# A decoder layer's output projection in pairs of token blocks by Strassen's product, with the layer norm on three engines

## The chip, the core and the metric

The kernel runs on one core of a Trainium2 chip. A core has TensorE (PE, with PEld for its weight loads), VectorE (DVE), ScalarE (ACT), GpSimd (POOL) and SyncE (SP, which here only issues DMAs). The metric is the device time of one execution in microseconds; it is 440.44 us before the change, the median of three runs (439.75 to 440.67).

## What is computed

One decoder layer for 1024 tokens of width 1024, all in float32. Cut to what matters:

```python
h = x @ w_in                                  # 1024 x 2368: six parts
x_q, x_kv, k_rope_raw, gate_a, u_pool, gate_b = split(h)
y_a = latent_attention(x_q, x_kv, k_rope_raw, positions, ...) * silu(gate_a)   # 4 heads, causal by position
y_b = pooling_mixer(u_pool, pool_w, pool_scale) * silu(gate_b)                 # windows 2, 4, 8, 16
mix = concatenate([y_a, y_b], axis=-1) @ w_out                                 # 1024 x 1024
x = layer_norm(alpha * x + mix, ln_g, ln_b)
```

The causal mask is by `positions`; where they rise strictly, a block of queries needs only the blocks of keys up to its own.

## The kernel before

**Precision.** Every matrix product is made of three fp32r matmuls: an operand is split into a high part (cast to fp32r, on ACT: `split`, line 419) and a low part (the rest, on DVE or, with `pool=True`, on POOL: `low`, line 415), and high·high, high·low and low·high are summed in PSUM. A split of a tile is thus one ACT cast and one subtraction.

**Stages.** `start` (line 373) loads positions, weights and x and makes a flag that says whether positions rise; the program branches on it (line 1277). The fast branch runs `in_projection` (with `gate_a` first), `up_projections`, `attention` and `out_projection`. The input projection already goes by Strassen's product in Winograd's form: eight rounds, each of which makes two column tiles from seven products of 12 matmuls (`multiply`, line 535); sums of x's quarters are made once (`right_sums`), sums of w_in's tiles in each round (`prepare`), and round i asks for the weights of round i+2 and prepares those of round i+1. The mixer's results go to DRAM (`yb_d`), as does silu of the gates (`silu_d`).

**Order.** Nothing is issued where it is written. Each call notes an operation in a `Planner` (line 86), which, before the build, lays out all operations of the branch by a list schedule: each engine takes, of what is ready within 30 ns of the soonest, what is written first, by costs set in `cost` (line 141). That fixes each engine's order and which buffer each tile gets: 13 pages of 128 x 1024 float32 (`F`, named m), 41 of the same size for split operands and others (`T`, named b), and six places in PSUM (`PS_KINDS`, a set for each stage). Tiles of a kind are handed out in the order of first use; a later one can go ahead only if enough are spare for all before it. All instructions therefore carry one line in the profile, L316, and groups are told by tile names and shapes.

**Output projection.** `out_projection` (line 1222) takes eight blocks of 128 tokens. For blocks 0 to 3 it goes through the eight row tiles of w_out (`wo_split`: load, split) and adds to four accumulators; then blocks 4 to 7 come one after the other. Per block and row tile `out_mm` issues three terms by two halves of 512 columns. The last block's second half is cut into two of 256. When a block is summed, `norm` (line 1179) does on DVE: alpha·x + sum, statistics, aggregate, epsilon; the power -1/2 on POOL; a centring and a scaling pass of 1024 on DVE; the store. The last block does these two passes in four pieces, one of which is scaled by ACT and POOL. During attention, `SIDE_AT` names the steps at which y_b's four tiles and w_out's first three are split, with the low parts on POOL.

Of the kernel before, what the change touches and what calls it, by code (L numbers as in the profile page):

```python
# [33 lines left out]
SIDE_AT = (9, 12, 16, 28, 20, 22, 29)  # L34
# [9 lines left out]
}  # L44
# [297 lines left out]
class Layer:  # L342
    def __init__(self, ctx, tc, d, out, plans):
# [20 lines left out]
        self.trig_d = dram.tile([32, 2, S], F32, name="trig_d")  # L364
        self.yb_d = [dram.tile([P, S], F32, name=f"yb_d{i}") for i in range(4)]
# [77 lines left out]
    def bank(self):  # L443
        kind = ("a1", "x1", "p1")[self.stage]
        return self.E.tile(self.ps, kind, len(PS_KINDS[kind][1]), [P, 512], F32)
# [11 lines left out]
    def run(self, ctx, full):  # L457
# [10 lines left out]
        E.tracked = {t.tensor.name for t in self.silu_d + self.yb_d + [self.trig_d]}  # L468
# [381 lines left out]
    def in_projection(self):  # L850
# [8 lines left out]
        for i, (n, _) in enumerate(self.PAIRS):  # L859
# [119 lines left out]
    def attention(self):  # L979
# [3 lines left out]
        self.ya, self.yb, self.wo, self.wo_raw = [None] * NH, [None] * NH, [None] * 8, {}  # L983
# [100 lines left out]
        def pv(h, g):  # L1084
# [12 lines left out]
            if self.ya[h] is None:  # L1097
                self.ya[h] = (self.T(), self.T())
            c = slice(g * GQ * 128, g * GQ * 128 + GQ * 128)
            y = self.silu_a[h][:, c]  # L1100
            self.mul(y, ps, y)
            self.split(self.ya[h][0][:, c], self.ya[h][1][:, c], y, pool=True)

        side = {}
        if not full:
            side = {}
            for t, job in zip(SIDE_AT, [(self.yb_split, g) for g in range(4)] + [(self.wo_split, n) for n in range(3)]):
# [37 lines left out]
        if full:  # L1145
            for g in range(4):
                self.yb_split(g)

# [7 lines left out]
    WO_ORDER = (4, 5, 6, 7, 0, 1, 2, 3)  # L1156

    def yb_split(self, g, pool=False):
        y = self.load(self.yb_d[g])
        self.yb[g] = (self.T(), self.T())  # L1160
        self.split(*self.yb[g], y, pool)

    def wo_split(self, n, pool=False):
        k = self.WO_ORDER[n]
        raw = self.load(self.d["w_out"][k])
        self.wo[k] = (self.T(), self.T())
        self.split(*self.wo[k], raw, pool)

    def out_mm(self, parts, s, n):
        k = self.WO_ORDER[n]  # L1170
        a, w = self.ya[k] if k < 4 else self.yb[k - 4], self.wo[k]
        for q, (i, j) in enumerate(((0, 0), (0, 1), (1, 0))):
            for f, c in parts:
                self.E.tensor.matmul(
                    f, a[i][:, s * 128 : s * 128 + 128], w[j][:, c],
                    start=(n == 0 and q == 0), stop=(n == 7 and q == 2),
                )

    def norm(self, s, parts, tail=False):
        E, small, ln_g, ln_b = self.E, self.small, self.ln_g, self.ln_b  # L1180
        z, o = self.xs.pop(s), self.F()
        b0 = 48 + 16 * (s % 2)
        mv, rs = small[:, b0 : b0 + 2], small[:, b0 + 2 : b0 + 3]
        stats = self.stats[:, 18 * (s % 2) : 18 * (s % 2) + 18]
        i = 0
        for f, c in parts:
            E.vector.scalar_tensor_tensor(out=o[:, c], in0=z[:, c], scalar=ALPHA, in1=f, op0=ALU.mult, op1=ALU.add)
            for n in range(c.start, c.stop, 512):
                E.vector.bn_stats(out=stats[:, 6 * i : 6 * i + 6], in_=o[:, n : min(n + 512, c.stop)])
                i += 1  # L1190
        E.vector.bn_aggr(out=mv, in_=stats[:, : 6 * i])
        E.vector.tensor_scalar(out=rs, in0=mv[:, 1:2], scalar1=LN_EPS, scalar2=None, op0=ALU.add)
        E.gpsimd.tensor_tensor(out=rs, in0=rs, in1=self.half[:, 0:1], op=ALU.pow)
        def center(c):
            E.vector.scalar_tensor_tensor(
                out=z[:, c], in0=o[:, c], scalar=mv[:, 0:1], in1=ln_g[:, c], op0=ALU.subtract, op1=ALU.mult
            )

        def scale(c, pool=False):
            if pool:  # L1200
                E.scalar.activation(o[:, c], z[:, c], AF.Identity, scale=rs)
                E.gpsimd.tensor_tensor(out=o[:, c], in0=o[:, c], in1=ln_b[:, c], op=ALU.add)
            else:
                E.vector.scalar_tensor_tensor(
                    out=o[:, c], in0=z[:, c], scalar=rs, in1=ln_b[:, c], op0=ALU.mult, op1=ALU.add
                )
            E.sync.dma_start(self.out[s * 128 : s * 128 + 128, c], o[:, c])

        if not tail:
# [12 lines left out]
    def out_projection(self):  # L1222
        E = self.E
        self.ln_g, self.ln_b = self.F(), self.F()
        E.sync.dma_start(self.ln_g, self.d["ln"][0:1, :].partition_broadcast(128))
        E.sync.dma_start(self.ln_b, self.d["ln"][1:2, :].partition_broadcast(128))
        self.xs = {}

        def x_load(s):
            if s < NB:  # L1230
                self.xs[s] = self.load(self.d["x"][s * 128 : s * 128 + 128, :])

        for s in range(3):
            x_load(s)
        accs = [self.acc() for _ in range(4)]
        for n in range(8):
            if n >= (0 if self.full else 3):
                self.wo_split(n)
# [126 lines left out]
```

## Time and profile before

| | |
|---|---|
| median of three runs | 440.44 us |
| the profiled execution, its own time | 439.69 us |
| its span, first to last instruction | 437.9 us |
| mean granted TensorE clock | 0.988 |
| PE busy | 424.9 us, 97% of the span, 2031 matmuls |
| DVE busy | 325.9 us, 74% |
| ACT busy | 187.1 us, 43% |
| POOL busy | 74.9 us, 17% |
| HBM read, written | 31.81 MB, 8.65 MB |
| PE's share of the chain that ended last | 87% |

Busy time is the time in which an engine had an instruction in work. Idle time of an engine that is not on the chain that ended last costs nothing by itself. Matmuls are pipelined, so their single durations overlap; a pitch is read from a stretch, as time over count. The same holds for DVE's short passes: the start of one to the start of the next is their pitch.

### The profile page before, as it was taken

The numbers are of one execution on the slowest core, as the hardware profiler recorded it, in microseconds if no ns is written. First come the engines' busy times: TensorE is split into PE (matmuls) and PEld (weight loads), VectorE is DVE, ScalarE is ACT, GpSimd is POOL, SyncE is SP. The second block draws the span as 40 slices with busy tenths as digits, with TensorE's granted clock in tenths as the row PEclk, the third lists the DMA queues.
The fourth block names the chain that finished last, engine by engine and source line by source line (L and its number), as shares of the span: only waits on it lengthen the run. The fifth ranks groups of instructions, "written<-read, shape, count | busy, mean of one in ns | idle before, by whom it ended". The sixth has DMA issues, their size and how long they took to land.

```text
span 437.9 us, 5669 instructions
## 1 busy us (share of the span) xinstructions
PE 424.9 (97%) x2031; PEld 356.4 (81%) x2031; DVE 325.9 (74%) x601; ACT 187.1 (43%) x338; POOL 74.9 (17%) x88
## 2 busy tenths in 40 slices
PE   6999999999999999999999999999999999999991
PEld 4888888888888888888788898989898888888881
DVE  4996996668688999838998679696969600299564
ACT  5755764243332436543333658596869200000000
POOL 0000001000010000000101116668483200024111
PEclk8999999999999999999999999999999999999996
DMA  8823522304023002514339101131447300032211
GB/s 287 334 97 99 214 100 93 97 0 145 0 105 101 0 23 66 179 63 128 120 79 214 68 1 49 50 97 52 157 144 265 106 1 0 0 136 106 96 49 56
DMA packets 14457, 43.53 MB, mean 99 GB/s; under 512 B 2133, under 2 KB 4309, under 8 KB 14421
## 3 DMA queue, kind: packets, MB, share of 16 engines
q1 hardware_dynamic: 14133, 42.57, 29.4%
q10 hardware_dynamic: 288, 0.52, 0.4%
q8 instruction: 18, 0.29, 0.3%
q14 instruction: 18, 0.15, 0.1%
HBM read 31.81 MB, written 8.65 MB: 92 GB/s over the span
## 4 chain that ended last, share of the span: by engine, by line
PE 87%; DVE 6%; DMA 4%; ACT 1%; issue 1%; DVEq 0%
PE p L316 49%; PE x L316 31%; PE a L316 7%; DVE m L316 3%; DMA m<-w_uq 3%; DVE b L316 2%; DMA pp<-pos_pair 1%; DVE small L316 1%; ACT m L316 0%; ACT b L316 0%; DVEq L400 0%; DVE stats L316 0%; DVE p L316 0%; PE psflag L396 0%; DVE cmp L389 0%
## 5 line engine op out<-in xcount | busy, mean ns | idle before, releaser
L316 PE MATMUL p<-b,b 128*128 128x512 f32 (+4 forms) x1032 | 220.9, 370 | 0.1
L316 PEld LDWEIGHTS p<-b,b 128*128 128x128 f32 x1032 | 181.2, 188 | 30.2 <-DVE b L316 0.4
L316 PE MATMUL x<-b,b 128*128 128x512 f32 x696 | 158.2, 389 | 0.0
L316 PEld LDWEIGHTS x<-b,b 128*128 128x128 f32 x696 | 130.6, 188 | 27.4 <-ACT m L316 0.4
L316 ACT CAST b<-m 128x1024 fp32r<-128x1024 f32 (+2 forms) x96 | 83.4, 898 | 51.3 <-DVE m L316 32.7
L316 DVE TENSOR_TENSOR b<-m,b 128x1024 fp32r<-128x1024 f32 (+3 forms) x91 | 84.2, 963 | 17.9 <-ACT b L316 17.8
L316 ACT CAST b<-p 128x256 fp32r<-128x256 f32 (+3 forms) x118 | 37.3, 385 | 29.8 <-PE p L316 29.5
L316 DVE TENSOR_TENSOR b<-p,b 128x256 fp32r<-128x256 f32 (+3 forms) x118 | 44.0, 419 | 6.2 <-ACT b L316 6.0
L316 DVE SCALAR_TENSOR_TENSOR m<-m,p 128x512 f32<-128x512 f32 (+2 forms) x13 | 10.2, 799 | 43.4 <-PE p L316 43.4
L316 POOL TENSOR_TENSOR small<-small,cst 128x1 f32<-128x1 f32 (+1 forms) x10 | 14.8, 1479 | 148.4 <-DVE small L316 148.4
L316 DVE TENSOR_TENSOR m<-m,m 128x512 f32<-128x512 f32 (+4 forms) x51 | 39.1, 788 | 1.4 <-ACT m L316 1.2
L316 ACT COPY m<-x 128x512 f32<-128x512 f32 x33 | 19.1, 586 | 48.5 <-PE x L316 41.4
L316 ACT ACTIVATE m<-m,small 128x320 f32<-128x320 f32 x1 | 0.6, 562 | 84.1 <-POOL small L316 84.1
L316 DVE TENSOR_TENSOR m<-m 128x512 f32<-128x512 f32 (+5 forms) x39 | 29.3, 761 | 4.7 <-ACT m L316 4.7
L316 POOL TENSOR_SCALAR m<-m,small 128x384 f32<-128x384 f32 (+7 forms) x32 | 24.0, 752 | 45.2 <-DVE small L316 36.8
L316 PE MATMUL a<-b,b 128*128 128x512 f32 x128 | 31.2, 406 | 0.3 <-DVE b L316 0.2
L316 PEld LDWEIGHTS a<-b,b 128*128 128x128 f32 x128 | 25.0, 197 | 6.3 <-DVE b L316 0.6
L316 ACT ACTIVATE m<-p,small 128x384 f32<-128x384 f32 (+7 forms) x32 | 26.7, 836 | 6.4 <-DVE small L316 5.9
L316 POOL COPY m<-m 128x1 f32<-128x1 f32 (+3 forms) x10 | 5.3, 535 | 137.3 <-DVE m L316 137.3
L316 POOL TENSOR_TENSOR b<-m,b 128x512 fp32r<-128x512 f32 (+1 forms) x15 | 27.2, 1826 | 8.8 <-ACT b L316 8.6
L316 DVE TENSOR_REDUCE small<-p 128x1 f32<-128x384 f32 (+7 forms) x32 | 24.2, 755 | 0.8
L316 DVE SCALAR_TENSOR_TENSOR m<-m,small,m 128x1024 f32<-128x1024 f32 (+3 forms) x21 | 21.3, 1035 | 1.4 <-POOL small L316 1.3
(59 smaller groups left out, 185.8 us busy)
## 6 DMA issues: line engine op xcount, KB each, us to landing
m<-w_in SPq DMA_DIRECT2D x16, 512.0 KB, 4.2
m<-w_out SPq DMA_DIRECT2D x8, 512.0 KB, 3.5
m<-x SPq DMA_DIRECT2D x8, 512.0 KB, 4.6
m<-xt SPq DMA_DIRECT2D x7, 512.0 KB, 6.7
out<-m SPq DMA_DIRECT2D x7, 512.0 KB, 2.6
silu_d<-m SPq DMA_DIRECT2D x4, 512.0 KB, 3.6
yb_d<-m SPq DMA_DIRECT2D x4, 512.0 KB, 2.6
m<-silu_d SPq DMA_DIRECT2D x4, 512.0 KB, 4.3
```

The costliest lines, as they stand in the source:

```text
L316: ins = fn(*args, **kw).ins
```

## The change

The eight token blocks of the output projection become four pairs, an even block e and an odd block o. With a11, a12 the even block's columns of y_a and y_b, a21, a22 the odd block's, and b the quarters of w_out (512 x 512 each), seven products stand for eight: a11·b11, a12·b21, a22·t4, s1·t1, s2·t2, s3·t3, s4·b22. Each is, per pair, 4 row tiles by 3 terms, 12 matmuls of 512 columns. The t are sums of w_out's quarters, the s sums of y's.

- `out_sums`, new, in rounds 2 to 5 of the input projection: loads two tiles of w_out, makes t1 to t4 for one row tile by four DVE subtractions, stores them to DRAM (`wt_d`).
- Attention: a11 only (the even blocks of y_a) is split; b21 and t4 of the four row tiles are loaded and split (`wo_first`) in place of w_out's first three.
- `out_projection`: b11 and t2 are loaded and split; a12·b21 and a22·t4 of all pairs; a11·b11 of all pairs, which stays in four PSUM banks; s1 to s4 of the four heads (`left_sums`: y_b loaded again, four DVE passes, two splits of a whole page each); t1, t3, b22 loaded and split; then per pair s2·t2 and s3·t3 on top of a11·b11's bank, s1·t1 and s4·b22 in another. Each result is added into z (x's block, scaled by alpha by the first addition to each half) by DVE.
- `norm` has three forms now. Blocks 0, 1 and 3: sum and sum of squares by two ACT passes with an accumulator, centring and scaling by ACT, times ln_g and plus ln_b by POOL, in halves. Blocks 2 and 4: sums by ACT, the passes by DVE. Blocks 5 and 7: statistics and passes by DVE as before. Block 6 is the last, with the pieces of the old tail. z is changed in place, so no second page is used.
- `start`: the two halves of x's first block go out on SP behind the positions and the first block of w_ga, not on ACT; `gate_a` has three warm-up matmuls, not two.

The diff, cut to its core:

```diff
-SIDE_AT = (9, 12, 16, 28, 20, 22, 29)
+SIDE_AT = (9, 12, 16, 28, 20, 22, 25, 29)
+WO_AT = (2, 3, 4, 5)
...
+    "o1": (3, (2, 3, 4, 5, 0, 1)),
...
-        for c in (slice(0, 512), slice(512, 1024)):
-            nc.scalar.dma_start(m[0][:, c], d["xt"][0][:, c])
         nc.sync.dma_start(self.pp, d["pos_pair"].rearrange("a p t -> p a t"))
         for k in range(KD):
             nc.sync.dma_start(self.w_first(k), d["w_ga"][k])
-            if k:
-                nc.sync.dma_start(m[k], d["xt"][k])
+            for c in [slice(0, 512), slice(512, 1024)] if k == 0 else [slice(0, 1024)]:
+                nc.sync.dma_start(m[k][:, c], d["xt"][k][:, c])
...
-        for _ in range(2):
+        for _ in range(3):
             E.tensor.matmul(accs[1].bank(1)[:, 0:256], self.warm[:, 0:128], self.warm, start=True, stop=True)
...
+            if i in WO_AT:
+                self.out_sums(WO_AT.index(i))
...
+    def out_sums(self, k):
+        lo, hi = slice(0, 512), slice(512, 1024)
+        a, b = self.load(self.d["w_out"][k]), self.load(self.d["w_out"][k + 4])
+        r, s = self.F(), self.F()
+        self.sub(r[:, lo], a[:, hi], a[:, lo])
+        self.sub(r[:, hi], b[:, hi], r[:, lo])
+        self.sub(s[:, lo], b[:, hi], a[:, hi])
+        self.sub(s[:, hi], r[:, hi], b[:, lo])
+        self.E.sync.dma_start(self.wt_d[k][:, 0:1024], r)
+        self.E.sync.dma_start(self.wt_d[k][:, 1024:2048], s)
...
+    def left_sums(self, h):
+        yb, ya = self.T(F32), self.silu_a[h]
+        self.E.sync.dma_start(yb, self.yb_d[h])
+        a11, a21, a12, a22 = self.blocks(ya, 0), self.blocks(ya, 1), self.blocks(yb, 0), self.blocks(yb, 1)
...
+        (r1, r2), (s3, s4) = views[0][0], views[1][0]
+        self.add(r1, a21, a22)
+        self.sub(r2, r1, a11)
+        self.split(*views[0][3])
+        self.sub(s3, a11, a21)
+        self.sub(s4, a12, r2)
+        self.split(*views[1][3])
...
+    def norm(self, s, n, how="vector"):
...
+        else:
+            t, total = self.T(F32), small[:, b0 + 4 : b0 + 6]
+            E.scalar.activation(t, z, AF.Identity, accum_out=total[:, 0:1])
...
+            E.scalar.activation(t, z, AF.Square, bias=neg, accum_out=total[:, 1:2])
...
+        if how == "gpsimd":
+            E.vector.tensor_scalar(out=neg, in0=neg, scalar1=rs, scalar2=None, op0=ALU.mult)
+            for c in (slice(0, 512), slice(512, 1024)):
+                E.scalar.activation(z[:, c], z[:, c], AF.Identity, bias=neg, scale=rs)
+                E.gpsimd.tensor_tensor(out=z[:, c], in0=z[:, c], in1=ln_g[:, c], op=ALU.mult)
+                E.gpsimd.tensor_tensor(out=z[:, c], in0=z[:, c], in1=ln_b[:, c], op=ALU.add)
+                E.sync.dma_start(self.out[s * 128 : s * 128 + 128, c], z[:, c])
+            return
...
+        for a, b, odd, op in (("a12", "b21", 0, ALU.add), ("a22", "t4", 1, ALU.subtract)):
+            for p in (0, 2):
+                ps = E.tile(self.ps, "p2", 2, [P, 2, 512], F32)
+                for q in (p, p + 1):
+                    s = 2 * q + odd
+                    self.z[s] = self.load(self.d["x"][s * 128 : s * 128 + 128, :])
+                    self.product(ps[:, q - p, :], a, b, q)
+                    residual(s, lo, ps[:, q - p, :], op)
...
+        for p in range(4):
+            e, o = 2 * p, 2 * p + 1
+            self.product(x[p], "s2", "t2", p, False)
+            residual(e, hi, x[p], ALU.add)
...
+                self.product(f, "s1", "t1", p, True, c)
+                residual(o, slice(512 + c.start, 512 + c.stop), f, ALU.add)
+            self.product(x[p], "s3", "t3", p, False)
+            for i, c in enumerate((lo, hi)):
+                self.add(self.z[o][:, c], x[p], self.z[o][:, c])
...
+            if p < 2:
+                self.norm(o, 0, "gpsimd")
+                self.last(p, y[p])
+                self.norm(e, 0, "vector" if p else "gpsimd")
+            elif p == 2:
+                self.norm(5, 2)
+        self.bn(6, 0, lo)
+        self.norm(7, 2)
+        self.last(2, y[2])
+        for i, (f, c) in enumerate(y[3]):
+            self.last(3, [(f, c)])
+            self.bn(6, i + 1, slice(512 + c.start, 512 + c.stop))
+        self.norm(4, 0)
+        self.norm(6, 3, "tail")
```

`last(p, ...)` is the product s4·b22 of pair p and its addition into the even block's second half; `product` issues the 12 matmuls.

## Rows read from the trace of the kernel before

**Rows 1.** windows: us, busy (x) by engine, granted clock, DMA share, GB/s

```profile
80.00:140.00 60.00, 60.00 (x266) 49.71 (x265) 43.65 (x59) 22.27 (x28) 2.59 (x7) 1.00 0.20 64
140.00:172.00 32.00, 32.00 (x143) 26.51 (x142) 32.00 (x62) 14.01 (x20) 0.51 (x2) 1.00 0.10 36
184.00:192.00 8.00, 8.00 (x37) 6.60 (x37) 1.97 (x2) 2.48 (x4) 0.00 (x0) 1.00 0.22 89
...
360.00:380.00 20.00, 20.00 (x90) 16.55 (x89) 0.00 (x0) 0.00 (x0) 0.00 (x0) 1.00 0.00 0
```

**Rows 2.** chain that ended last: start us, us, what

```profile
312.88 115.68 PE p L316 x579
...
432.87 0.48 DVE m L316
```

**Rows 3.** timeline of the start: start us, us, engine, line, operation

```profile
0.73 0.88 ACTq L377 DMA_DIRECT2D m<-xt  x2
0.74 0.39 SPq L378 DMA_DIRECT2D pp<-pos_pair  x1
...
1.18 0.86 SPq L380 DMA_DIRECT2D m<-w_ga  x2
...
4.70 0.17 DVE L389 TENSOR_TENSOR cmp<-pp 93x11 f32<-93x11 int32 x1 [3.70 <-DMA pp<-pos_pair]
...
6.15 1.50 ACT L316 CAST b<-m 128x512 fp32r<-128x512 f32 x3 [3.02 <-DVE flag L399]
```

**Rows 4.** DMA issues by line: count, KB each, median us from issue to landing

```profile
m<-w_out SPq DMA_DIRECT2D x8, 512.0 KB, 3.5
...
m<-xt ACTq DMA_DIRECT2D x2, 256.0 KB, 4.6
...
m<-pos SPq DMA_DIRECT2D x4, 32.0 KB, 1.8
```

**Rows 5.** timeline of DVE in the input projection, three instructions in a row

```profile
59.79 0.68 DVE L316 TENSOR_TENSOR m<-m,m 128x512 f32<-128x512 f32 x1
60.39 1.21 DVE L316 TENSOR_TENSOR b<-m,b 128x1024 fp32r<-128x1024 f32 x1
61.53 0.68 DVE L316 TENSOR_TENSOR m<-m 128x512 f32<-128x512 f32 x1
```

**Rows 6.** timeline at the end of attention, all engines

```profile
340.25 1.08 ACT L316 CAST b<-m 128x1024 fp32r<-128x1024 f32 x1
...
341.99 3.44 DVE L316 TENSOR_TENSOR b<-m,b 128x1024 fp32r<-128x1024 f32 x2
...
342.81 1.54 POOL L316 TENSOR_TENSOR b<-m,b 128x512 fp32r<-128x512 f32 x1 [5.45 <-ACT b L316]
345.35 0.68 DVE L316 TENSOR_TENSOR m<-p,m 128x512 f32<-128x512 f32 x1
```

**Rows 7.** timeline of DVE in the output projection

```profile
390.97 1.27 DVE L316 SCALAR_TENSOR_TENSOR m<-m,small,m 128x1024 f32<-128x1024 f32 x1
392.15 0.69 DVE L316 BATCH_NORM_STATS2 stats<-m 128x6 f32<-128x512 f32 x1
...
428.58 0.42 DVE L316 SCALAR_TENSOR_TENSOR m<-m,p 128x256 f32<-128x256 f32 x1 [1.99 <-PE p L316]
...
429.77 0.15 DVE L316 TENSOR_SCALAR small<-small 128x1 f32<-128x1 f32 x1
429.84 3.51 DVE L316 SCALAR_TENSOR_TENSOR m<-m,small,m 128x320 f32<-128x320 f32 x7
```

**Rows 8.** timeline of POOL in the output projection

```profile
385.09 1.54 POOL L316 TENSOR_TENSOR small<-small,cst 128x1 f32<-128x1 f32 x1 [37.03 <-DVE small L316]
...
430.00 0.79 POOL L316 TENSOR_TENSOR small<-small,cst 128x1 f32<-128x1 f32 x1 [8.03 <-DVE small L316]
```

**Rows 9.** windows of the whole core at the start, columns as in Rows 1

```profile
3.00:7.00 4.00, 1.98 (x12) 0.93 (x11) 1.12 (x5) 0.98 (x3) 0.00 (x0) 1.00 0.94 329
...
8.00:11.00 3.00, 3.00 (x8) 2.33 (x8) 3.00 (x8) 2.79 (x6) 0.00 (x0) 0.50 1.03 406
```

More of the change, by code (lines that the diff above doesn't have):

```diff
@@ L1106, in attention @@
             side = {}
-            for t, job in zip(SIDE_AT, [(self.yb_split, g) for g in range(4)] + [(self.wo_split, n) for n in range(3)]):
+            for t, job in zip(SIDE_AT, [(self.yb_split, g) for g in range(4)] + [(self.wo_first, k) for k in range(4)]):
                 side.setdefault(t, []).append(job)
@@ L1147, in attention @@
                 self.yb_split(g)
+                self.wo_first(g)
     def pt_tile(self, pt, key):
@@ L1158, in yb_split @@
     def yb_split(self, g, pool=False):
         y = self.load(self.yb_d[g])
[L1160 to L1173, printed above, removed]
+        h, l = self.T(), self.T()
@@ new lines, in yb_split, with right_part @@
+        self.split(h, l, y, pool)
+        for i, name in enumerate(("a12", "a22")):
+            self.left[name, g] = (self.blocks(h, i), self.blocks(l, i))
+    def right_part(self, k, names, raw, pool=False):
+        w, t = self.d["w_out"], self.wt_d[k]
+        src = {"b11": w[k][:, 0:512], "b21": w[k + 4][:, 0:512], "b22": w[k + 4][:, 512:1024]}
+        src.update({f"t{i + 1}": t[:, i * 512 : i * 512 + 512] for i in range(4)})
+        for i, name in enumerate(names):
+            c = slice(i * 512, i * 512 + 512)
+            self.E.sync.dma_start(raw[:, c], src[name])
+        if pool:
+            h, l = self.T(), self.T()
+            self.split(h, l, raw, True)
+        for i, name in enumerate(names):
+            c = slice(i * 512, i * 512 + 512)
+            if pool:
+                self.right[name, k] = (h[:, c], l[:, c])
+            else:
+                x = self.T()
+                self.right[name, k] = (x[:, 0:512], x[:, 512:1024])
+                self.split(*self.right[name, k], raw[:, c])
@@ L1174, in out_mm, with product @@
+    def product(self, bank, a, b, p, first=True, cols=slice(0, 512)):
+        for k in range(4):
+            for s, (i, j) in enumerate(((0, 0), (0, 1), (1, 0))):
                 self.E.tensor.matmul(
-                    f, a[i][:, s * 128 : s * 128 + 128], w[j][:, c],
-                    start=(n == 0 and q == 0), stop=(n == 7 and q == 2),
-                )
-    def norm(self, s, parts, tail=False):
-        E, small, ln_g, ln_b = self.E, self.small, self.ln_g, self.ln_b
[L1181 to L1192, printed above, removed]
-        E.gpsimd.tensor_tensor(out=rs, in0=rs, in1=self.half[:, 0:1], op=ALU.pow)
@@ L1225, in out_projection @@
+        self.stage = 3
+        x = []
+        for p in range(4):
+            x.append(self.bank())
+            self.product(x[p], "a11", "b11", p)
+            self.add(self.z[2 * p][:, lo], x[p], self.z[2 * p][:, lo])
+        for h in range(NH):
+            self.left_sums(h)
+        for names in (("t1", "t3"), ("b22",)):
+            for k in range(4):
+                self.right_part(k, names, self.T(F32))
         E.sync.dma_start(self.ln_g, self.d["ln"][0:1, :].partition_broadcast(128))
@@ L1226, in out_projection @@
         E.sync.dma_start(self.ln_b, self.d["ln"][1:2, :].partition_broadcast(128))
[L1227 to L1238, printed above, removed]
-            for s in range(4):
-                self.out_mm(accs[s].banks, s, n)
-                if n == 7:
-                    self.norm(s, accs[s].parts)
-                    x_load(s + 3)
@@ L1244, in out_projection @@
-        for s in range(4, NB):
-            if s < NB - 1:
-                acc = self.acc()
-                for n in range(8):
-                    self.out_mm(acc.banks, s, n)
-                self.norm(s, acc.parts)
-                x_load(s + 3)
-            else:
-                parts = [(self.bank(), slice(0, 512))]
-                parts += [(self.bank()[:, 0:256], slice(c, c + 256)) for c in (512, 768)]
-                for part in parts:
-                    for n in range(8):
-                        self.out_mm([part], s, n)
-                self.norm(s, parts, tail=True)
+        y = {}
@@ L1260, in plan, with last @@
+        self.bn(6, 0, lo)
[6 more added lines that the diff above has]
+        self.norm(6, 3, "tail")
+    def last(self, p, parts):
+        for f, c in parts:
+            self.product(f, "s4", "b22", p, False, c)
+            z = self.z[2 * p][:, 512 + c.start : 512 + c.stop]
+            self.add(z, f, z)
 def plan(parts, full):
```

80 lines of the change are left out of this document (66 added, 14 removed).

## The prediction

> **What bounds the kernel now.** I read the busy time by stretch first. In every stretch between the start and the tail TensorE (PE) is busy for all of the time, while VectorE (DVE) has idle room in some stretches and none in others; the reader is to see that both facts hold side by side [rows 1]. Then the chain of waits: its last long piece is 115.68 us of PE without a break, and the last matmul ends at 312.88 + 115.68 = 428.56 us; what follows to the last row at 432.87 + 0.48 = 433.35 is DVE [rows 2]. So a matmul taken out anywhere before 428.56 shortens the time by its pitch, as long as nothing else comes late, and work added to DVE is free where DVE idles and dear in the last microseconds. Then the DVE, GpSimd (POOL) and DMA rows of the places that the change touches.
>
> The profiled execution took 439.69 us, 1.79 more than its span of 437.9, and stands 0.75 under the median of 440.44. The sum is made against 439.69 and 0.75 is put back.
>
> **The matmuls of the output projection.** Before: 8 blocks x 8 row tiles x 3 terms x 2 halves = 384 matmuls of 512 columns, 24 of them cut into 48 of 256. After: 7 products x 4 pairs x 4 row tiles x 3 terms = 336, and again 24 are cut into 48 (the last pair's s1·t1 and s4·b22). So 48 whole matmuls go. The pitch in this stage is 20.00 us / 90 = 0.222 us [rows 1]: 48 x 0.222 = **10.7 us less**. Both ends of the doubt are near: the weight loads are busy 16.55 of 20 us for 89 of them, 0.186 each, under 0.222, so chains that change the stationary block at every matmul do not lengthen the pitch.
>
> **The start.** Today the two halves of x's first block go out on ScalarE's (ACT's) queue at 0.73, beside the positions at 0.74 on SP's; DVE takes the positions at 4.70, and by way of the flag ACT casts x's first half at 6.15 [rows 3]. After the change the positions go alone, and behind them, on SP, w_ga's first block and then the halves. Small loads in calmer stretches land in 1.8 us [rows 4], the positions took 4.70 - 0.74 = 3.96: the most that can be won is some 2.1 us. On the other side the first half, which takes 4.6 us to land [rows 4], so arrived near 5.3, is issued about 0.9 us later (two issues of SP, 0.39 and 0.43 each, go ahead of it), which puts it at 6.2 if nothing else changes: just too late for 6.15, some 0.1 to 0.5 lost, with the second half after it. I take half a microsecond of DMA crowding less, hence 5.5 for the half, and a flag as early: **0.6 less**. The weights and x blocks behind stand in the same order as before, one or two issues later; ACT takes each as it lands while PE spends 16 matmuls on a block, so they are covered. The third warm-up matmul, 0.4 us at most (a whole matmul of 512 columns at half the clock), runs while PE waits for ACT and DVE.
>
> **The sums of w_out in the input projection.** Four times two loads of 512 KB, four DVE subtractions of 512 columns, two stores. A subtraction costs 0.60 us (59.79 to 60.39), a low part of 1024 columns 1.14 (60.39 to 61.53) [rows 5]: 16 x 0.60 = 9.6 us of DVE. From 80 to 140 us DVE is busy 43.65 of 60 us, 16.3 us free, which holds three of the four sums (7.2 us). From 140 to 172 it has no room at all [rows 1]; the fourth falls there, and everything DVE does then ends up to 2.4 us later, until the idle 6 us of 184 to 192 take it up. The DMA share of 80 to 140 is 0.20 at 64 GB/s, so 8 MB more go beside it. On SP the stores wait for the subtractions, and the loads of w_in queue behind them; the code asks for those one round ahead of DVE's use and two ahead of PE's (a round is 84 matmuls, 18.7 us), and SP's 16 new issues take some 0.4 us each. The same queueing holds for the 13 f32 tiles: each sum takes four for about 10 us (landing 3.5 [rows 4], four subtractions 2.4, storing as long as landing). Bounds: 0, and 10 us if no round had such tiles to spare; nearest the idle rows, I take **0.5 more**.
>
> **Attention.** The high and low parts of y_a are now cast for the even blocks alone (half the columns of eight casts and eight POOL subtractions), against one more w_out job (a cast and a POOL subtraction of 1024 columns). POOL's 512-column row is 1.54 [rows 6], so eight halves save some 6 us and the job costs about 3. PE sets this stage. Bounds: 0, and 3 if that job stood in PE's way; POOL gains on balance, so I take 0.
>
> **The middle of the output projection.** Let T be the virtual start of its matmuls, 428.56 - 384 x 0.222 = 343.3. Products a12·b21, a22·t4 and a11·b11 take 144 matmuls, 32.0 us; s2·t2 of the first pair needs the last head's s1 and s2 at T + 34, about 377. Today DVE's last act before the norms is the product of 345.35 [rows 6], and from 360 to 380 it does nothing [rows 1]; that is the cover. The new demand on it: eight residuals and four additions 12 x 0.60 = 7.2; the left sums, per head four of 512 and two low parts of 1024, 4 x 0.60 + 2 x 1.14 = 4.7, four heads 18.7. That is 25.9 us from 346 to 377, 31 us. The low parts of t1 and t3, 8 x 0.60 = 4.8, have to come by T + 36.7 = 380. So 30.7 us of work stand against 34: DVE turns from idle to 90% busy and just keeps up. (The eight low parts of b11 and t2, 4.8 us, take the place of w_out's last five, 5.7 us, at the end of attention.) Tiles: of the 41 one-page tiles 20 hold a11, a12, a22 and b21/t4, eight b11 and t2; 13 are left, a head's sums keep four of seven, so three heads fit before the tiles of the first 96 matmuls come free at T + 21.3 = 364.6. Bounds: 0, and the wait of the third rival; I take **0.5 more**.
>
> **The norms and the tail.** From one pair to the next DVE has little to do (five passes, 3.0 us in 10.7). But blocks 7, 4 and 6 now all end in the last microseconds, where before block 6 ended 11 us ahead of block 7. Count from the end of the matmuls: s3·t3 of the last pair ends 24 x 0.222 = 5.3 us before. Then on DVE: block 7's two additions and two statistics 4 x 0.60, aggregate and epsilon 2 x 0.15, centre 1.18 (390.97 to 392.15 [rows 7]), block 4's addition 0.60, block 7's scale 1.18, half an addition and its statistics 0.84: 6.5 us, so 1.2 of it lies behind the last matmul. Block 4 then has its two passes of 1.18 and three small instructions of 0.15 left, 2.8 us, since its mean and variance are made by two ACT passes (a cast of 1024 columns takes 1.08 [rows 6]) one after the other and a power on POOL. Block 6's own tail is as before, 428.58 to 433.35 [rows 7]. Together 4.0; a little of the small work fits into the wait for POOL's power: **3.8 more**. Bounds: 1.5, if all but block 4's second pass falls into holes; 6.0, if the stores of blocks 7 and 4 (512 KB each) crowd the last pieces.
>
> What takes a place on POOL: three norms of four passes, 12 x 1.54 = 18.5 us between about 383 and 410, ahead of the powers of blocks 5, 7, 4 and 6. Here rows show a collision: two low parts on DVE take 3.44 us at 341.99 instead of 2.3, with POOL's subtraction from 342.81 to 344.35 in between [rows 6], and POOL's power takes 1.54 us at 385.09 beside DVE's long passes, 0.79 at 430.00 [rows 8]. [...]
>
> **Sum:** 439.69 - 10.7 - 0.6 + 0.5 + 0.5 + 3.8 = 433.2; with 0.75, **433.9 us**.
>
> **The rivals.** *The clock comes back early* (15%). [...]
>
> *POOL and DVE block each other into the tail* (10%). If the last gpsimd norm's four passes still run when block 7's passes begin, each shuts out DVE for up to 1.54: two of them, 3.1, give 437.0. [...]
>
> *The left sums wait for tiles* (9%, the slower side). If attention still holds the tiles, all four heads' sums begin at 364.6: 18.7 + 2.4 of additions + 2.4 of t1 and t3 in between make 388 against 377, 11 us: 433.9 - 0.5 + 11 = 444.4. It decides at about 6.5 us, two and a half heads late. For it: 41 tiles and 28 in use; against: 13 free by my count, and DVE idle from 346.
>
> *The count falls but not the time* (4%): if PE waited elsewhere for what it gains, 440.4. Against: PE's row has no hole to fall back on [rows 1].
>
> **The numbers.** My forecast has 62%; its own range is 431.5 to 436 by the bounds above. The range reaches from the cured clock with a small tail, 429.8, to a DVE that comes 5 us late in the middle, 438.6. About 0.2% is what a measurement of this kernel can tell. Faster 0.87, same 0.04, slower 0.09.
>
> **What would show it.** The x-named and p-named matmuls 48 fewer, PE's last matmul near 418; DVE busy in nine tenths of 346 to 380; the cast of x's first half near 5.5; behind PE's last matmul 8 to 9 us of DVE instead of 4.8. Wrong if PE idles for over 2 us anywhere between 8 and 417, or if the tail is as short as before.

## The result, and the profile after

The changed kernel takes 435.19 us, median of 4 runs (434.29 to 435.81), beside 440.36 (439.75 to 440.67, 4 runs) for the kernel before on the same chip: ratio 0.9891 [0.9875, 0.9908]. That is faster by more than 0.2%, 1.3 us above the forecast of 433.9 and inside its range. The profiled execution took 434.82 us with a span of 433.0, against 439.69 and 437.9. One execution of e6 below, 436.34 us beside a fastest of 429.81, counts as slow and is left out of its figures.

Cut at two points, the end of stage a (the first matmuls of the input projection, those of `gate_a`, named a in the profile) and the last matmul of all, the two spans and the forecast compare so:

```
                               before   after   change   forecast
stage a ends at                 38.22   37.42    -0.80      -0.6
from there to PE's last matmul 390.34  380.83    -9.51      -9.7
behind PE's last matmul          9.34   14.75    +5.41      +3.8
span                            437.9   433.0     -4.9      -6.5
```

Two of the three terms came out near their sums, the first of them by luck, as the part on the prediction shows; the tail is the one that was mis-sized. First the windows of the kernel after (us; busy time and count of PE, weight loads, DVE, ACT and POOL; granted clock; DMA share; GB/s), which answer to [rows 1]:

```profile
80.00:140.00 60.00, 60.00 (x267) 49.69 (x266) 47.93 (x61) 20.91 (x28) 2.76 (x7) 1.00 0.44 143
140.00:172.00 32.00, 32.00 (x143) 26.51 (x142) 32.00 (x66) 13.19 (x18) 1.76 (x2) 1.00 0.41 148
...
184.00:192.00 8.00, 8.00 (x37) 6.64 (x36) 5.00 (x6) 5.18 (x7) 0.00 (x0) 1.00 0.43 152
...
192.00:215.00 23.00, 22.59 (x99) 18.05 (x98) 20.32 (x23) 9.71 (x12) 1.65 (x1) 1.00 0.32 103
...
346.00:380.00 34.00, 32.70 (x143) 26.42 (x142) 32.85 (x46) 15.38 (x20) 1.13 (x1) 1.00 0.43 140
...
360.00:380.00 20.00, 20.00 (x90) 16.57 (x89) 18.88 (x28) 11.38 (x16) 0.00 (x0) 1.00 0.57 185
```

DVE took three of the four sums of w_out in 80 to 140 with room to spare (their stores go out from 94.13 to 140.98). The fourth fell where DVE has no room, and what it pushed back was taken up behind: in 184 to 192 DVE is busy for 5.00 us instead of 1.97. DVE went from nothing to 18.88 of 20 us in 360 to 380; PE stayed full there. PE is idle for 0.41 us in 192 to 215 (0.20 before) and for 1.30 in 346 to 380. The start, answering to [rows 3] (timeline: start, us, engine, line, operation, count, and what the wait before it was for):

```profile
2.72 0.17 DVE L390 TENSOR_TENSOR cmp<-pp 93x11 f32<-93x11 int32 x1 [1.71 <-DMA pp<-pos_pair]
...
4.75 0.62 ACT L318 CAST b<-m 128x512 fp32r<-128x512 f32 x1 [2.53 <-DMA m<-xt]
...
7.77 0.98 ACT L318 CAST b<-m 128x320 fp32r<-128x320 f32 x2 [2.40 <-DMA m<-w_ga]
...
8.79 28.63 PE L318 MATMUL a<-b,b 128*128 128x512 f32 x125 [1.92 <-ACT b L318]
```

The positions are there 1.98 us sooner than before and the first cast stands at 4.75 instead of 6.15. Then a new wait eats it up: in ACT's planned order the cast of w_ga's second block stands ahead of that of x's second half, and ACT waits 2.40 us for that block. PE waits behind it, and its long run starts at 8.79, where before it started at 7.76:

```profile
7.76 30.46 PE L316 MATMUL a<-b,b 128*128 128x512 f32 x126 [0.21 <-DVE b L316]
```

The run is 1.83 us shorter than before, only 0.22 of which is the one matmul fewer. The rest, 1.61, goes with the clock, granted 1.00 in 8 to 12 us where before it was 0.59 (0.41 of 4 us is 1.64), and the part on the prediction comes back to it.

The tail on DVE, answering to [rows 7], and on POOL, answering to [rows 8]:

```profile
409.11 1.59 DVE L318 SCALAR_TENSOR_TENSOR m<-m,small,m 128x1024 f32<-128x1024 f32 x1
...
412.39 1.28 DVE L318 SCALAR_TENSOR_TENSOR m<-m,small,m 128x1024 f32<-128x1024 f32 x1 [1.36 <-POOL small L318]
...
413.92 1.28 DVE L318 TENSOR_TENSOR m<-o,m 128x512 f32<-128x512 f32 x2
...
423.17 2.28 DVE L318 SCALAR_TENSOR_TENSOR m<-m,small,m 128x1024 f32<-128x1024 f32 x2
425.89 2.20 DVE L318 SCALAR_TENSOR_TENSOR m<-m,small,m 128x1024 f32<-128x1024 f32 x3 [0.44 <-POOL small L318]
```

```profile
392.55 11.05 POOL L318 TENSOR_TENSOR m<-m,m 128x512 f32<-128x512 f32 x8 [0.28 <-ACT m L318]
...
405.35 6.50 POOL L318 TENSOR_TENSOR m<-m,m 128x512 f32<-128x512 f32 x4 [0.72 <-ACT m L318]
411.81 0.54 POOL L318 TENSOR_TENSOR small<-small,cst 128x1 f32<-128x1 f32 x1
...
423.21 1.95 POOL L318 TENSOR_TENSOR m<-m,m 128x320 f32<-128x320 f32 x1 [0.67 <-ACT m L318]
```

Block 5's centre pass is done at 410.7. Its power waits in POOL's queue behind four passes of the third POOL norm, so its scale comes at 412.39, and block 7's additions, whose product ended 24 x 0.222 = 5.3 us before PE's last matmul at 418.25, so at 412.9, start a microsecond late. DVE ends at 428.09, 9.8 us behind PE; before it was 4.8.

### The profile page after: what moved, and what is told of

Same layout as the page of the kernel before. It is cut to its first block, busy times and chain, and to the rows that moved or that the text cites. A ratio compares the mean times of both kernels' runs of the same rounds, so it can differ in the third digit from the quotient of the medians.

```text
span 433.0 us, 5838 instructions
## 1 busy us (share of the span) xinstructions
PE 412.7 (95%) x1984; PEld 346.0 (80%) x1984; DVE 359.2 (83%) x666; ACT 217.0 (50%) x388; POOL 87.6 (20%) x101
## 4 chain that ended last, share of the span: by engine, by line
PE 70%; DVE 14%; DMA 7%; POOL 4%; issue 2%; ACT 1%; SPq 1%; POOLq 0%; DVEq 0%; ACTq 0%
PE p L318 30%; PE x L318 27%; DVE m L318 8%; PE a L318 7%; PE o L318 6%; DVE b L318 4%; POOL m L318 4%; DMA m<-trig_d 3%; DMA m<-w_ga 1%; DMA b<-w_out 1%; DMA b<-yb_d 1%; DVE small L318 1%; ACT m L318 1%; POOLq L1482 0%; DVE stats L318 0%
## 5 line engine op out<-in xcount | busy, mean ns | idle before, releaser
L318 PE MATMUL p<-b,b 128*128 128x512 f32 (+4 forms) x720 | 155.1, 369 | 1.3 <-DVE m L318 1.3
L318 PEld LDWEIGHTS p<-b,b 128*128 128x128 f32 x720 | 125.6, 188 | 21.2 <-DVE m L318 2.1
L318 ACT CAST b<-m 128x1024 fp32r<-128x1024 f32 (+3 forms) x92 | 77.7, 871 | 47.4 <-DVE m L318 31.8
L318 DVE TENSOR_TENSOR b<-m,b 128x1024 fp32r<-128x1024 f32 (+4 forms) x90 | 80.0, 925 | 10.0 <-ACT b L318 9.8
L318 PE MATMUL o<-b,b 128*128 128x512 f32 (+1 forms) x264 | 55.1, 370 | 0.0
L318 PEld LDWEIGHTS o<-b,b 128*128 128x128 f32 x264 | 46.4, 188 | 8.6 <-DVE m L318 0.2
L318 DVE TENSOR_TENSOR m<-m,m 128x512 f32<-128x512 f32 (+4 forms) x63 | 47.2, 770 | 2.5 <-ACT m L318 1.6
L318 ACT CAST b<-b 128x512 fp32r<-128x512 f32 (+1 forms) x28 | 20.2, 748 | 20.7 <-DVE b L318 11.1
L318 POOL TENSOR_TENSOR b<-m,b 128x1024 fp32r<-128x1024 f32 (+1 forms) x16 | 26.2, 1638 | 11.0 <-ACT b L318 10.0
L318 DVE TENSOR_TENSOR b<-b,b 128x512 fp32r<-128x512 f32 (+2 forms) x32 | 24.9, 823 | 1.8 <-ACT b L318 1.5
```

The costliest lines, as they stand in the source:

```text
L318: ins = fn(*args, **kw).ins
```

## The experiments

All are measured beside the kernel before on their own chip, in three groups. What decides them is one table over the profiled executions: the end of stage a, PE's last matmul, and the span behind it, with PE's granted clock in 8 to 12 us and its idle time in two stretches. Each row is one execution; the medians below are of several.

```
                       clock  stage a  idle     idle     last    behind
                       8-12   ends     192-215  340-366  matmul  it
before                 0.59   38.22    0.20     0.00     428.56   9.34
as changed             1.00   37.42    0.41     1.30     418.25  14.75
e10, the same again    0.59   38.80    0.27     2.50     420.72  14.8
e1, start of before    1.00   37.93    0.05     1.04     418.01  14.8
e2, cast order         1.00   35.78    0.04     1.75     417.30  14.8
e9, tables late        1.00   36.30    0.00     1.71     416.96  14.7
e11, e2 and e9         1.00   35.95    0.00     1.02     416.22  14.8
e3, last2, norm 4      1.00   36.92    1.42     2.51     421.92  12.6
e3b, last2 alone       1.00   36.54    1.21     1.77     420.71  12.6
e4, block 3 on DVE     1.00   37.47    1.82     1.55     422.48  13.8
e5, right part, POOL   0.57   38.49    0.27     2.63     420.35  14.8
e6, no norm of 4       0.50   40.11    0.00     1.48     420.70  11.4
e12, POOL priced       0.59   37.99    0.05     1.07     418.10  14.5
e13, e2, e9 and e12    1.00   35.99    0.00     1.88     417.00  14.5
```

**The start (e1, e2).** The first puts back the start of before (x's halves on ACT's queue ahead, two warm-up matmuls); the second changes one expected time in the plan, so that ACT casts x's second half first.

```diff
-                ((k % 3) * 320, (k % 3) * 320 + 320, 4700.0 if k < 2 else 4600.0 + 1720.0 * k)
+                ((k % 3) * 320, (k % 3) * 320 + 320, 4700.0 if k < 1 else 4600.0 + 1720.0 * k)
```

e1: 

> The changed kernel (435.2 us) with the start of before put back: x's first halves on ACT's queue ahead of the positions, two warm-up matmuls. Theory A (the start gives what the trace shows where the input projection's first matmuls end, 37.42 instead of 38.22 us, and some 0.1 to 0.2 of it is lost again before 214): this kernel takes 0.6 to 0.9 more, 435.8 to 436.1, the positions land near 4.7 us and the granted clock falls to 0.5 between 8 and 12 us. Rival B (what is won at the start is taken back by DVE's backlog at 214): no difference, 435.1 to 435.4. If the clock alone were what the start changes, 1.5 to 1.9 more: 436.7 to 437.1.

Measured: 435.63 us (434.55 to 437.25), ratio 0.9909 [0.9889, 0.9929]. That lies between the ranges of A and B: the new start is worth some tenths at most and is not told from nothing by these intervals. The fall of the clock that was expected with the old start is not on record in its profile.

e2: 

> The changed kernel with one number of the plan changed: w_ga's second block is expected at 6.3 us, not 4.7, so that ACT casts the second half of x's first block before it, not behind it; a few instructions of the first block change their order, nothing else. Theory A: PE's wait of 1.92 us at 6.87 to 8.79 is ACT's queue: the second half has landed and stands behind a cast that waits until 7.77 for w_ga's block. Then the wait shrinks to under 1 us and the kernel takes 0.8 to 1.5 less, 433.7 to 434.4. Rival B: the half itself lands only near 7.7, as all loads share one bandwidth; then under 0.5 less, 434.7 to 435.2. Rival C: PE starts sooner at the lower clock; no gain.

Measured: 434.01 us (433.21 to 434.15), 0.9858 [0.9839, 0.9878]. ACT and PE in e2:

```profile
6.26 0.98 ACT L318 CAST b<-m 128x512 fp32r<-128x512 f32 x2 [0.48 <-DMA m<-xt]
...
6.93 28.85 PE L318 MATMUL a<-b,b 128*128 128x512 f32 x126 [0.37 <-ACT b L318]
```

The 1.92 us wait is 0.37 now, and stage a ends at 35.78, as theory A has it. The wait was ACT's order and not the landing of x: the second half is there for a cast at 6.26.

**The tables' loads (e9).** In the profile after, the chain of waits has `184.44 14.75 DMA m<-trig_d`: two table loads of 512 KB take that long where the plan reckons with 332 GB/s. e4's trace shows what a late one costs:

```profile
201.01 1.22 DVE L318 TENSOR_TENSOR m<-m,m 64x1024 f32<-64x1024 f32 x1 [2.33 <-DMA m<-trig_d]
```

```diff
-        o.move = 4 * self.cols(writes[0]) * writes[0].ap[0][1] / 332.0 if eng == "sync" else 0
+        o.move = 4 * self.cols(writes[0]) * writes[0].ap[0][1] / 332.0 * (5 if any("trig_d" in v.tensor.name for v in reads) else 1) if eng == "sync" else 0
```

> The changed kernel (435.2 us) with one number of the plan changed: the loads of the sine and cosine tables are expected to take five times as long (the trace shows 14.75 us), so that DVE does the split of the key-value squares before the first product with the cosines, not behind it. Theory A: w_out's sums delay these tables from 174 to 184 us, the wait for them stands in DVE's queue ahead of what PE needs at 201 us, and it differs from one execution to the next (0.65 us in one trace, 2.33 in another, where PE then idles 1.8): this kernel takes 0.5 to 1.5 less in the median, 433.7 to 434.7, and its executions lie closer together. Rival B: the wait is hidden as a rule; no difference in the median, 435.0 to 435.6.

Measured: 434.16 us (433.25 to 435.36), 0.9875 [0.9851, 0.99]. DVE takes other work first, PE's idle time in 192 to 215 is 0 in the three profiles with this price (e9, e11, e13) and up to 1.82 us in those without it; the interval overlaps that of the kernel as changed, so alone it settles nothing.

**Order and owner of the norms (e3, e3b, e4).** e3 and e3b put the last product of pair 2 (`last(2)`) ahead of pair 3, e3 with block 4's norm right behind it; e4 gives block 3's norm from POOL to DVE. The three edits in one view, cut:

```diff
             elif p == 2:
                 self.norm(5, 2)
+                self.last(2, y[2])
+                self.norm(4, 0)      # e3; in e3b behind pair 3
-        self.last(2, y[2])
-        self.norm(4, 0)
-                self.norm(o, 0, "gpsimd")
+                self.norm(o, 0, "vector" if p else "gpsimd")   # e4 alone
```

e3: 

> The changed kernel with the third pair's last product (s4.b22) and block 4's norm moved ahead of the fourth pair, as for the first two pairs; the same instructions. Theory A (the tail of 9.85 us of DVE behind the last matmul is the passes of blocks 7, 4 and 6 that end together): block 4's addition, two passes and small work, some 3.4 us, go from behind the last matmul to in front of it, and block 7's sums come 2.7 us later in PE's order, so that some 2.5 of its passes stay behind: the tail falls by 1 to 2.5 us, the time to 432.7 to 434.2. Rival B (the tail is held by POOL, whose last four passes keep the power of block 5 back until 412.35): block 4's power waits too, DVE's backlog only moves, 434.7 to 435.7. Slower, 436 and more, if block 7's norm now ends last.

e3b: 

> The third pair's last product moved ahead of the fourth pair, as in the run before, but block 4's norm is written behind the fourth pair's sums, so that DVE takes its passes only where it is idle. Theory A (there the gain in the tail, some 2.2 us, was given back because DVE did block 4's and block 5's passes before the fourth pair's residual and PE waited 1.69 us for it): PE's wait goes to under 0.5 and the tail stays short; 432.9 to 434.2. Rival B (DVE's whole work of the last 25 us binds, in whatever order): the passes of block 4 come back behind the last matmul and the time is that of the changed kernel, 434.8 to 435.6.

e4: 

> The changed kernel with block 3's centring and scaling on DVE (two passes of 1024) in place of ACT and POOL (four POOL passes of 512, seen at 405.35 to 411.85). Theory A (POOL and DVE block each other, and block 5's scale waits until 412.39 for its power behind POOL's passes): the power comes some 3 us sooner, block 7's additions start near 412.6 and not 413.92, and the tail is 0.8 to 1.5 us shorter: 433.7 to 434.4. Rival B (DVE's sum of work binds from 400 on): two more passes, 2.4 us, push the tail out by 0.5 to 2.4: 435.7 to 437.6.

Measured: e3 436.49 us (434.36 to 437.95), 0.9915 [0.9887, 0.9943]; e3b 435.23 (432.55 to 436.16), 0.9881 [0.9847, 0.9914]; e4 435.75 (433.07 to 438.42), 0.9893 [0.9857, 0.9929]. e3 and e3b cut the span behind the last matmul to 12.6, and PE pays most of it back; DVE and PE in e3b:

```profile
412.88 1.28 DVE L318 SCALAR_TENSOR_TENSOR m<-m,small,m 128x1024 f32<-128x1024 f32 x1 [1.58 <-POOL small L318]
414.09 1.01 DVE L318 SCALAR_TENSOR_TENSOR m<-m,o 128x512 f32<-128x512 f32 x2
```

```profile
414.82 5.89 PE L318 MATMUL o<-b,b 128*128 128x512 f32 x36 [1.73 <-DVE m L318]
```

DVE stands 1.58 us for the same late power, with the reading of PE's bank queued behind it, and PE waits 1.73. e4 takes a microsecond off the tail (13.8), since block 5's scale is out of the way when block 7's product ends; but PE waits 0.74 us for a DVE that now does block 3. The times of e3b and e4 lie in the ranges of their rivals B, though the tails shrank as theory A has it: in e3b nothing came back behind the last matmul. No version is told from the kernel as changed.

**POOL beside DVE in the middle (e5).**

```diff
-            self.right_part(k, ("b11", "t2"), self.T(F32))
+            self.right_part(k, ("b11", "t2"), self.T(F32), k == 3)
```

> The changed kernel with the low parts of the last row tile of b11 and t2 made by POOL, which idles there, not by DVE. Theory A (PE's waits of 0.35 and 0.94 us between 348 and 355 come from DVE's queue: DVE waits 1.53 us at 344.04 for a cast whose load was issued at 338.27 and took 5.04 us, and the residuals that free PE's accumulators stand behind it): the waits shrink by 0.7 to 1.3, 433.9 to 434.5. Rival B (DVE simply has too much to do from 344 to 364, 96% busy): the waits shrink by no more than the two low parts are worth and PE still waits 0.8 or more: 434.7 to 435.3. Worse, if POOL's long pass shuts DVE out.

Measured: 440.23 us (436.32 to 441.96, 12 runs), 0.9997 [0.997, 1.0024]: the whole gain is gone. The place in the trace of e5:

```profile
345.61 2.39 POOL L318 TENSOR_TENSOR b<-b,b 128x1024 fp32r<-128x1024 f32 x1 [2.99 <-DMA b<-yb_d]
345.75 2.80 DVE L318 TENSOR_TENSOR b<-m,b 128x512 f32<-128x512 f32 x1 [0.29 <-DMA b<-yb_d]
...
350.33 1.89 PE L318 MATMUL p<-b,b 128*128 128x512 f32 x7 [1.72 <-DVE m L318]
```

A DVE pass of 512 columns, 0.68 us for the same form in the profile after, started 0.14 us behind POOL's of 2.39, takes 2.80 and ends 0.55 after it. PE then waits 1.72, where it waited 0.35 in the profile after; but in e10 it waits 1.56 at the same place without that pass, so what the pass alone costs PE is not shown. The profiled execution, 436.9, idles 1.3 us more in the middle than the one after; what its slower executions, up to 441.96, lose beyond that, no trace shows.

**Block 4's norm (e6).** Block 4 is written out without its layer norm.

```diff
-        self.norm(4, 0)
+        E.sync.dma_start(self.out[512:640, :], self.z.pop(4))
         self.norm(6, 3, "tail")
```

> The changed kernel without block 4's norm: its rows are stored as the residual sums, neither centred nor scaled (left out: two ACT passes, three small DVE instructions, a power on POOL, two DVE passes of 1024). It prices one norm in the tail. Theory A (DVE's sum of work behind the last matmul sets the end): 2.4 to 3.2 less, 432.0 to 432.8, and the tail of DVE falls from 9.85 to some 7 us. Rival B (block 4's passes fill holes of block 6's tail): under 1.2 less, 434.0 to 435.2.

Measured: 433.89 us (429.81 to 434.48, 5 runs), 0.9845 [0.9804, 0.9885]. DVE's last rows in e6:

```profile
423.97 0.15 DVE L318 TENSOR_SCALAR small<-small 128x1 f32<-128x1 f32 x1
424.04 3.51 DVE L318 SCALAR_TENSOR_TENSOR m<-m,small,m 128x320 f32<-128x320 f32 x7
```

DVE ends at 427.55, 6.85 behind PE (as changed 9.84), and 4.55 before the span ends (as changed 4.91, before 4.55). So block 4's norm costs 3.0 us of DVE and 0.36 of its store. The span of this execution fell by 0.9 us only, mainly because its stage a ended 2.69 us later: its granted clock was 0.50 in all of 8 to 12 us. The median lies between the two ranges; the tail bears out theory A.

**All causes side by side on one chip (e10 to e13).** e10 is the kernel as changed once more; e11 joins e2 and e9; e12 prices POOL's 128x512 passes in the plan at the 1.63 us that block 3's took (6.50 us for four); e13 has all three.

```diff
-        return 148 + 2.105 * c
+        return 1630.0 if method == "tensor_tensor" and c == 512 else 148 + 2.105 * c
```

e10: 

> The changed kernel once more, nothing altered, as the measure for the three kernels beside it on this chip. All theories: 434.3 to 435.8 us, 14.7 to 14.8 us of span behind the last matmul (its order is fixed), and a spread of about 1.5 us between executions that comes from PE's waits ahead of it: 0.3 to 1.9 us behind the first half of x, 0 to 1.8 us at the in-projection's late tables, 1.0 to 1.9 us at the start of the output projection. If instead the tail differs from execution to execution, the span behind the last matmul leaves 14.5 to 15.0.

e11: 

> Both alterations of the plan at once: the cast of the weights' second block expected after x's second half, and the tables' loads expected five times as slow. Theory that the executions differ by PE's waits at these two places: the two gains add, so 432.9 to 433.7 us and a spread under 1 us; stage a ends by 36.0 and PE is idle under 0.2 us in 192 to 215. Rival, that PE's lead is lost later anyway (the output projection's right-hand parts set its start): 434.0 to 435.0, and PE's idle time in 340 to 366 grows from 1.3 to over 2 us.

e12: 

> The plan is told that POOL's 128x512 passes take 1.63 us (as measured beside DVE) where it reckoned 1.23; DVE's order in the tail alone changes, block 7's sum passes standing ahead of block 5's scale. Theory that the term for the tail was too small because DVE stood waiting 1.36 us for block 5's power, queued behind those passes: that wait goes to under 0.3 us, the span behind the last matmul shrinks by 1.0 to 1.4 us to 13.3 to 13.8, time 433.6 to 434.4. Rival, that DVE's backlog is work alone and stretched passes, so the wait only moves (to PE's last products or to POOL's later power): 14.3 us or more behind the last matmul, and a time as of the kernel as changed within 0.4 us.

e13: 

> All three alterations together. If the three are separate places on one path, their gains add: 431.6 to 432.8 us. If the tail's rival holds (its wait only moves) 432.9 to 433.7, as with the first two alone; if PE's lead is lost at the start of the output projection, 433.5 or more.

Measured, beside 439.58 us (438.7 to 440.93) for the kernel before: e10 436.85 (433.48 to 439.04, 8 runs), 0.9926 [0.9894, 0.9959]; e11 433.07 (432.4 to 433.3, 5 runs), 0.985 [0.9829, 0.9871]; e12 435.59 (434.29 to 436.95), 0.9915 [0.9891, 0.9939]; e13 433.25 (433.01 to 434.86), 0.9864 [0.984, 0.9888].

e10's expectation was too narrow: the changed kernel's executions scatter over 5.6 us. In every profile whose tail is left as it was, it is 14.7 to 14.8, so what scatters lies ahead of the last matmul: e10's profile loses 1.38 us against the earlier one in stage a, where PE's run is 1.58 us longer with a clock of 0.59 instead of 1.00 in 8 to 12 us, and 1.20 more in 340 to 366. That second loss is a load. DVE stands in its order for ACT's cast of b11's last row tile; its load was issued at 338.27 in the profile after and cast at 343.38, and at 339.28 and 345.60 in e10. DVE and PE, first as changed, then in e10:

```profile
344.04 0.69 DVE L318 TENSOR_TENSOR b<-b,b 128x512 fp32r<-128x512 f32 x1 [1.53 <-ACT b L318]
348.33 5.75 PE L318 MATMUL p<-b,b 128*128 128x512 f32 x24 [0.35 <-DVE m L318]
```

```profile
346.25 0.69 DVE L318 TENSOR_TENSOR b<-b,b 128x512 fp32r<-128x512 f32 x1 [2.73 <-ACT b L318]
350.53 5.75 PE L318 MATMUL p<-b,b 128*128 128x512 f32 x24 [1.56 <-DVE m L318]
```

It does not follow the late start: e6 ends stage a last and idles 1.48 us there, e2 ends it first and idles 1.75. Why the load takes longer in one execution than in another stays open.

e11 beats both kernels, and its interval lies apart from e10's; its five executions lie within 0.9 us. In the table, the nine kernels with the changed start and its cast order end stage a anywhere from 36.30 to 40.11; the three with the new order from 35.78 to 35.99. Four of the nine had the lower clock; the other five end it from 36.30 to 37.47. So the cast order, not the position of the loads, makes the start good, by 0.3 to 1.7 us; how much of the evenness is the order's and how much the clock's is not shown. e13 takes as long as e11, as the rival has it for a tail whose wait only moves.

e12 refutes my theory of the tail as I had put it. Its DVE:

```profile
410.16 0.74 DVE L318 SCALAR_TENSOR_TENSOR m<-m,o 128x256 f32<-128x256 f32 x2
412.55 1.29 DVE L318 TENSOR_TENSOR m<-o,m 128x512 f32<-128x512 f32 x2 [1.65 <-PE o L318]
413.75 0.68 DVE L318 BATCH_NORM_STATS2 stats<-m 128x6 f32<-128x512 f32 x1
414.42 1.28 DVE L318 SCALAR_TENSOR_TENSOR m<-m,small,m 128x1024 f32<-128x1024 f32 x1
...
422.71 4.90 DVE L318 SCALAR_TENSOR_TENSOR m<-m,small,m 128x1024 f32<-128x1024 f32 x6
```

The wait for POOL is gone and block 7's additions start the moment their product ends; DVE now waits for PE in the same hole, and block 5's scale (414.42) falls behind that point, where DVE is busy without a break until 427.61. That shortens the tail by 0.25 us, not 1.0 to 1.4. The wait was a sign; the cost is that the scale of block 5, 1.2 us of work, misses the hole before 412.5, whichever instruction stands first.

## Why the prediction was right, and where it was off

**The matmuls: right.** 48 fewer and one warm-up more (2031 to 1984), PE's last matmul at 418.25 where "near 418" was forecast (at 420.72 in e10). The matmuls and the two terms of 0.5 for in-projection and middle were to give -9.7 and gave -9.51. The waits are small and stand where they were put, with other sizes than 0.5 and 0.5: 0.2 us more behind the in-projection, where DVE waits 0.65 us for the tables of sines, a load that I had not priced, and 1.30 in the middle of the output projection. With 10.7 less for the matmuls that makes -9.2; the last 0.3 stays open.

**The start: right in size by luck, wrong in make-up.** -0.80 measured, -0.6 forecast. But PE's long run starts 1.03 us later than before, and ends earlier only because, with a clock of 1.00 instead of 0.59 in 8 to 12 us, it was 1.6 us shorter, and the change is not shown to set the clock. With as much of the lower clock as the profile before had (0.57 to 0.59 in 8 to 12 us), the changed start ends stage a at 37.99 (e12), 38.49 (e5) and 38.80 us (e10), where before it was 38.22: nothing is won on the whole. So 1.6 of the 4.9 us between the two spans are not the change's. The cast came at 4.75 (5.46 in e10) where 5.5 was forecast; the 1.92 us wait behind it was not in the prediction, though it was readable: it said of ACT that it "takes each as it lands", and the plan's order does not let it. The diff leaves the plan's expected landing times alone, and with them the order, while the landings had moved.

**The tail: right in kind, 1.6 us too small.** e6 splits the 5.4 us: 3.35 for block 4's norm, where 2.8 was counted and 0.2 of it hoped into a hole (the 0.36 of its store was left to the range), and 2.06 of backlog, where 1.2 was counted. Of block 4's 3.0 us on DVE, 0.44 are the wait at 425.45 for block 4's own power, which stands on POOL (425.12) behind a pass of 320 columns; that pass took 1.95 us here and 1.09 in e6. For the backlog the failing step is the sentence that POOL's three norms run "between about 383 and 410", with nothing in the sum for the power of block 5 behind them. The twelve passes took 17.55 us, near the 18.5, but began at 392.55: ahead of them stand two ACT passes for each block, the powers and the first scaling, 8.6 us from the first block's last product, taken by DVE at 383.95. They ended at 411.85, and with them the power of block 5 came too late for DVE's last hole. e4, with four passes fewer on POOL, shows that microsecond (14.75 to 13.8).

**The rivals.** *The clock* came back in the profile after, as this rival has it, and hid the new wait at the start; but it is not shown to be the change that brings it. Granted clock in 8 to 12 us, before, as changed, and then in e10, which is the changed kernel again (windows, columns as above), with PE's run of stage a in e10:

```profile
8.00:12.00 4.00, 4.00 (x12) 3.10 (x12) 4.00 (x10) 3.55 (x8) 0.00 (x0) 0.59 1.04 409
```

```profile
8.00:12.00 4.00, 3.21 (x14) 2.67 (x15) 3.56 (x8) 3.48 (x8) 0.00 (x0) 1.00 1.02 399
```

```profile
8.00:12.00 4.00, 3.41 (x8) 2.68 (x9) 3.66 (x9) 3.37 (x8) 0.00 (x0) 0.59 1.02 390
```

```profile
8.59 30.21 PE L318 MATMUL a<-b,b 128*128 128x512 f32 x125 [1.23 <-ACT b L318]
```

In one execution of the changed kernel the granted clock was 1.00 in that stretch, in the other 0.59, the same fall as in [rows 9]; the same 125 matmuls of stage a took 28.63 and 30.21 us, 1.6 us apart. PE had been busy for 3.04 and 3.56 us of the five before, so the fuller stretch went with the lower clock. No run shows that a busier start brings the clock back: the cured clock in the lower end of the forecast's range, 429.8, was the author's estimate. Of the nine profiles with this start and cast order four show the lower clock (e5, e6, e10, e12), of the three with the new order none; that is too few to call the order a cure. e4's 125 matmuls took 29.84 us and e1's 128 took 30.97 though the clock on record is 1.00 there; why stays open. In e10's eight executions the mean granted clock falls from 0.989 at 433.48 us to 0.981 at 439.04, so the clock may have a part in that scatter; in e5 its slowest execution (441.96 us) has 0.989.

*POOL and DVE block each other*: seen in e5 (2.80 us instead of 0.68) and at 409.11, where a centre pass beside POOL's of 405.35 to 411.85 took 1.59 instead of 1.28, and smaller in the tail than the 3.1 us that the rival gave: with four POOL passes fewer (e4) the tail is 0.95 us shorter in all, and how that parts into blocking and the late power is not shown. *The left sums wait for tiles*: no; DVE was busy for 32.85 us of 346 to 380 and PE idle for 1.30. *The count falls but not the time*: no.

The forecast's own range, 431.5 to 436, holds the first median but not e10's 436.85, which only the wider range, up to 438.6, holds; and e10's two waits in the middle come to 2.50 us, more than the 2 that the prediction named as a sign of being wrong. That the executions scatter 2.5 times as far as those of before on the same chip (5.6 against 2.2 us) was not foreseen.

## What to carry to other kernels

Where one engine is full from start to end, count its instructions and trust the sum; put the care into the tail, and there ask for each piece of work not only how long it takes but when its first input can exist, by the whole chain through the other engines. When a load is moved earlier, look at what stands next to its consumer in that engine's fixed order: here one expected time in the plan was worth more than the moved load, and the executions with it lay closer together. Before a term is called right, compare the clock of the two profiles in that stretch: here a run of PE's that started 1.03 us later ended 0.80 sooner, with a clock of 1.00 instead of 0.59 in 8 to 12 us. And measure a kernel again before believing a difference of 1 us: the scatter of a kernel is a property that a change can alter.

## What the runs showed of the hardware

Two table loads of 512 KB each, written from 32 rows of memory to four groups of partitions, stand in the chain of waits with 14.75 us, where the loads of w_out and w_in, also 512 KB, land in 3.5 and 4.7 us; in 187 to 195 us, while they were under way, the DMA share was 0.26 to 0.27, a quarter of the 16 engines' time. POOL's power on a single column took 0.54 us while DVE stood waiting for it (411.81), and between 0.73 and 1.52 beside DVE's passes (421.75, 425.12, 416.98). The positions' load of 8 KB, which took 3.96 us beside two others, was there 1.98 us earlier when it went first, with the next load issued 0.43 us behind it (1.67 in e10). The same 125 matmuls took 28.63 us with a granted clock of 1.00 and 30.21 with 0.59 in 8 to 12 us, in two executions of one kernel.
